# V's tiles at multiples of 64 bytes in place of 32 bytes behind them, in one layer of a hybrid encoder

## The chip, the core and the metric

The kernel runs on one core of one Trainium2 chip. The metric is the device time of one execution in microseconds (us). Five engines of the core are named as the profile names them: PE (TensorE, matmuls; PEld is its loading of the stationary operand, the "weights"), DVE (VectorE), ACT (ScalarE), POOL (GpSimd) and SP (SyncE, which here only issues DMAs).

## What is computed

One layer of an encoder over 512 tokens of width 2,048, in float32. One projection of the normalised input gives queries (8 heads of 128), keys and values (2 heads of 128, each shared by four query heads), two gates and the input of a linear recurrence. Attention and recurrence run beside each other; both are normalised, gated, joined and projected back.

```python
def hybrid_layer(x, norm_w, w_in, ...):
    h = rms_norm(x, norm_w)
    proj = jnp.einsum('bsd,de->bse', h, w_in)
    q, k, v, g_attn, xr, g_lru = jnp.split(proj, SPLITS, axis=-1)
    attn_out = attention_group(q, k, v, q_norm_w, k_norm_w)
    lru_out = lru_group(xr, conv_w, conv_b, ...)
    mixed = jnp.concatenate([rms_norm(attn_out, attn_norm_w) * jax.nn.silu(g_attn),
                             rms_norm(lru_out, lru_norm_w) * jax.nn.silu(g_lru)], axis=-1)
    return x + jnp.einsum('bse,ed->bsd', mixed, w_out)
```

What the change touches is the second product of attention, softmax weights times V:

```python
    def block(qb):
        s = jnp.einsum('bkgqd,bksd->bkgqs', qb.astype(jnp.float32), k_t.astype(jnp.float32)) * scale
        p = jax.nn.softmax(s, axis=-1)
        return jnp.einsum('bkgqs,bksd->bkgqd', p, v_t.astype(jnp.float32)).astype(q.dtype)
```

## The kernel before

**Matmuls in three parts.** A float32 operand is split into a high part, rounded to the matmul's narrower float type (fp32r, also four bytes in memory), and a low part, the rest. A product is then three matmuls, high x high, high x low, low x high, summed in PSUM. The helper `mm3` (lines 152 to 155) issues them, so most matmuls of the profile stand on lines 153, 154 and 155, and the tiles' names tell them apart. The last projection issues its own on line 1026.

**Stages.** PE's order is written out by hand for the whole kernel: projections fill the gaps of whatever chain runs beside them (`weave`, line 423). First comes the projection of the recurrence's input, with x being turned (up to about 50 us); then the recurrence in two halves, with the gate maps of `lru_pair` (line 493: `gh`, `gl`, loaded as weights, profile names `mm<-k,k`); then keys, values and queries are evacuated and rotated (`kv`, line 655, and `norm_rope`, line 600); then attention (`attention`, line 760) beside the projections of the gates (`pj<-x,wh` and `pj<-x,wl`); then the output's product (line 1026). ACT, DVE and POOL follow an order that the framework works out from the dependences of the tiles and from priorities, except in the first part of the first stage and in the last; SP's order is by hand in the first stage, in attention and in the last.

**V.** `kv` takes four tiles `kv` of 128 tokens x 512 (K's two heads, then V's). For each of them it makes a tile of V (lines 661 to 664) with the high part in its first 256 columns and the low part in the other 256; ACT writes the high part (line 665) and DVE the low (line 666). These tiles are read in one place, `values` (line 731): for a head, four blocks of 128 tokens, three matmuls each, twelve in all, with a 128 x 128 block of V as the weights and the turned softmax weights (`ph`, `pl`) streaming past. Eight heads make 96 matmuls, `mm<-ph,v` and `mm<-pl,v` in the profile. Between the heads lie the scores (`mm<-kt,q`, line 699) and the gates' projections.

**Where tiles lie.** SBUF is laid out in two stacks of pools per partition, one from the left and one from the right. The right stack holds, from its end downwards, a small `pad`, two rings, and then one after another `lru` (closed at line 1250), `qkv` (opened at line 1252; `ev`, `lq`, `kt`, V), under it `wx` (opened in `kv`, line 658; four `wh` and four `wl`) and, when that is closed, `att` (line 1268; `p`, `q`, `u`, `ph`, `pl`, `pt` and small tiles). A tile's first writer waits for the last readers of the older tiles that lay in the same bytes. The left stack of that time holds `rope` (`rq`, `rk`, `kv`) and `rot` (`rr`, `sh`, `sq` and others), which `att` later reaches over. The slots of `lru` named `k2` hold 2,048 bytes each.

`aside(tile_of, n)` (line 854) asks for a tile that is 16 floats longer than n x 256 and hands back a view that starts 8 floats (32 bytes) in. V is the only tile that is made with it.

Of the kernel before, what the change touches and what calls it, by code (L numbers as in the profile page):

```python
# [12 lines left out]
F32R = mybir.dt.float32r  # L13
# [4 lines left out]
P = 128  # L18
# [3 lines left out]
NT = SEQ // P  # L22
HD = 128
NH = 8
NKV = 2
# [23 lines left out]
H = 256  # L49
# [14 lines left out]
def hybrid_kernel(  # L64
# [25 lines left out]
    pools, order = {}, {"left": [], "right": []}  # L90

    def opened(name, side):
        pools[name] = tc.alloc_tile_pool(name=name, bufs=1, side=side, reuse_waits="tile")
        order[side].append(name)
        return pools[name]
# [22 lines left out]
    def nm(s):  # L118
        cnt[0] += 1
        return f"{s}_{cnt[0]}"  # L120
# [28 lines left out]
    def f(ap):  # L149
        return ap.bitcast(F32)  # L150
# [201 lines left out]
    def rows(dst, col, dg):  # L352

        shape = [P, NT, P]
        part = [const([P, NT], nm("part")) for _ in range(2)]
        parts = [dg() for _ in part]
        nc.vector.tensor_copy(part[0].bitcast(F32R), col)
        nc.vector.tensor_sub(part[1], col, part[0])
        for c, d in zip(part, parts):
            nc.vector.tensor_mul(  # L360
                d, ident[:, None, :].broadcast_to(shape), c[:, :, None].broadcast_to(shape)
            )
        yield
        pb = mm()
        for k, d in enumerate(parts):
            d = d.rearrange("p t q -> p (t q)")
            nc.tensor.matmul(pb, ones_r, d, start=k == 0, stop=k == 1)  # L367
        nc.vector.tensor_copy(dst, pb)
        yield
# [59 lines left out]
    def drain(fill):  # L429
        for _ in fill:  # L430
            pass
# [128 lines left out]
    def lru_squares():  # L560

        hsum = pools["rot"].tile([P, 2, SEQ], F32, tag="hsum", name="hsum")
        nc.scalar.activation(hsum, hp[0], AF.Square)
        for pair in hp[1:]:
            yield 2
            sq = pools["rot"].tile([P, 2, SEQ], F32, tag="hsq", bufs=1, name=nm("hsq"))
            nc.scalar.activation(sq, pair, AF.Square)
            nc.vector.tensor_add(hsum, hsum, sq)
        sums["l"] = hsum[:, 0, :]
        nc.gpsimd.tensor_add(sums["l"], sums["l"], hsum[:, 1, :])  # L570
# [29 lines left out]
    def norm_rope(es, nh, tab):  # L600

        es = [e[:, : nh * HD].rearrange("p (h d) -> p h d", d=HD) for e in es]
        rs = []
        for e in es:
            r = pools["rot"].tile([P, nh], F32, tag=f"rr{nh}", bufs=NT, name=nm("rr"))
            for h in range(nh):
                sq = pools["rot"].tile([P, HD], F32, tag="sh", bufs=1, name=nm("sh"))
                nc.scalar.activation(sq, e[:, h, :], AF.Square, accum_out=r[:, h : h + 1])
            rsqrt_mean(r, r, HD, nh)
            rs.append(r)  # L610
        for t, (e, r) in enumerate(zip(es, rs)):
            sq = pools["rot"].tile([P, nh, HD], F32, tag="sq", bufs=2, name=nm("sq"))
            nc.vector.tensor_mul(e, e, r[:, :, None].broadcast_to([P, nh, HD]))
            for s in range(2):
                nc.vector.tensor_mul(
                    sq.rearrange("p h (a s d) -> p h a s d", s=2, d=32)[:, :, :, s, :],
                    e.rearrange("p h (a s d) -> p h a s d", s=2, d=32)[:, :, :, 1 - s, :],
                    tab[:, t, 1, :].rearrange("p (a s d) -> p a s d", s=2, d=32)[:, None, :, s, :]
                    .broadcast_to([P, nh, 2, 32]),
                )  # L620
            nc.vector.tensor_mul(e, e, tab[:, t, 0, :][:, None, :].broadcast_to([P, nh, HD]))
            nc.vector.tensor_add(e, e, sq)
        return es
# [7 lines left out]
    def sent(es, nh, *us):  # L631

        us = us or [
            pools["rot"].tile([P, NQ, 2, NT, B], F32, tag="uq", bufs=2, name=nm("uq"))
            for _ in range(nh // 2)
        ]
        for n, u in enumerate(us):
            for t, e in enumerate(es):
                blocks(u, t, e[:, 2 * n : 2 * n + 2].rearrange("p h d -> p (h d)"))
            yield  # L640
            asides.append(put_aside(u, "qd", 5))

    def landed(aside_):

        to = pools["qkv"].tile([P, NQ, 2, NT, B], F32, tag="lq", bufs=2, name=nm("lq"))
        bring_back(to, aside_)
        return to

    def split_head(pair, k, hi, lo):
        src = pair[:, :, k]  # L650
        hi, lo = (in_order(v) for v in (hi, lo))
        nc.scalar.copy(hi, src)
        nc.vector.tensor_sub(lo, src, f(hi))

    def kv(es):
        turned_k = sent(norm_rope(es, NKV, rk), NKV)
        yield 20
        opened("wx", "right")
        for t in range(NT):
            vv = es[t][:, NKV * HD :]  # L660
            vt = aside(
                lambda *a: pools["qkv"].tile(*a, tag="v", bufs=NT, name=nm("v")), 2 * NKV * HD // H
            )
            vh[t], vl[t] = vt[:, 0, :], vt[:, 1, :]
            nc.scalar.copy(vh[t], vv)
            nc.vector.tensor_sub(vl[t], vv, f(vh[t]))
        yield from lru_squares()
        yield 2
        drain(turned_k)
        yield 6  # L670
        pair = landed(asides.pop(0))
        for h in range(NKV):
            yield (12, 4)[h]
            kt = pools["qkv"].tile([P, 2, SEQ], F32R, tag="kt", bufs=NKV, name=nm("kt"))
            kth[h], ktl[h] = kt[:, 0, :], kt[:, 1, :]
            split_head(pair, h, kth[h], ktl[h])
        r = group_rstd(sums["l"], "r_l", NB * P)
        yield 4
        drain(rows(
            gbc, r,  # L680
            lambda: pools["rope"].tile([P, NT, P], F32R, tag="kv", bufs=NT, name=nm("kv")),
        ))
# [133 lines left out]
    def group_rstd(src, name, n):  # L816

        pr = mm()
        for t in range(NT):
            nc.tensor.matmul(  # L820
                pr[:, t : t + 1], src[:, t * P : (t + 1) * P], ones[:, 0:1], start=True, stop=True
            )
        r = const([P, NT], name)
        nc.vector.tensor_copy(r, pr[:, :NT])
        rsqrt_mean(r, r, n, NT)
        return r
# [15 lines left out]
    def seven(pair, hi, lo):  # L842
# [7 lines left out]
        for to, part in ((slice(0, 3), src[:, 1:4]), (slice(3, 7), res)):  # L850
            nc.scalar.copy(hi[:, to], part)
            nc.vector.tensor_sub(lo[:, to], part, f(hi[:, to]))

    def aside(tile_of, n):

        t = tile_of([P, n * H + 16], F32R)
        return t[:, 8 : 8 + n * H].rearrange("p (n e) -> p n e", e=H)

    def kept(pool, i):
        return [  # L860
# [339 lines left out]
    for step in proj_feat(C_XR, a1, first, given):  # L1200
# [8 lines left out]
        c, e = step  # L1209
# [51 lines left out]

    fill = with_sums(both(), 3)
    weave(fill, kv(kvs))
    drain(fill)

# [171 lines left out]
```

## Time and profile before

| | |
|---|---|
| median of 3 runs | 631.11 us (630.88 to 631.38) |
| the profiled execution | 631.51 us |
| its span, first to last instruction | 629.7 us |
| mean granted PE clock in it | 0.998 |
| PE busy / PEld busy | 623.8 / 514.4 us |
| DVE / ACT / POOL busy | 491.2 / 348.5 / 104.0 us |
| DMA moved | 127.61 MB, mean 203 GB/s |

The span is what the profile shows of the execution; the rest of the execution's time lies around it. Busy shares are means over stages with different limits. A row of a group reads: line, engine, operation, tile written <- tiles read, shape, count, then busy time and the mean of one in ns. Matmuls overlap: a record's end is modelled and lies behind the start of the next, so the pace of matmuls is the distance of their starts. A weight load (PEld) runs beneath the matmul before the one that it is for.

### The profile page before, as it was taken

Reading aid. Unit: us, or ns where it says so; the run is one execution under the profiler, and the core shown is the slowest. Engines: PE = TensorE matmul, PEld = TensorE weight load, DVE = VectorE, ACT = ScalarE, POOL = GpSimd, SP = SyncE. Lnnn points to the kernel's source line nnn. Section 1 sums busy time; section 2 is a strip of 40 time slices with the busy share of each in tenths; the row PEclk is TensorE's granted clock in tenths of the full one; section 3 lists DMA queues with packets and bytes.
Section 4 is the critical chain, followed back from the end, with each engine's and each line's share of the span. In section 5 each row is a group of like instructions: output and inputs, shape, how many; then the busy total and the mean of one; then the engine's idle time right before and its main releaser. Section 6 shows DMA issues by size and latency. Waiting matters only on the chain.

```text
span 629.7 us, 8304 instructions
## 1 busy us (share of the span) xinstructions
PE 623.8 (99%) x2771; PEld 514.4 (82%) x2771; DVE 491.2 (78%) x796; ACT 348.5 (55%) x612; POOL 104.0 (17%) x137
## 2 busy tenths in 40 slices
PE   9999999999999999999999999999999999999997
PEld 6888888888888888888888888888888888888885
DVE  5967979986699874987887888549978866886875
ACT  3764899379936812555475447435445633443441
POOL 0000210112003631622122232100310001010010
PEclk9999999999999999999999999999999999999999
DMA  8877676859774599489668646924995777896262
GB/s 286 286 225 235 176 195 174 177 137 194 235 233 135 170 250 233 100 209 272 190 166 250 201 142 192 263 72 130 238 236 187 212 251 243 286 320 235 68 200 100
DMA packets 73594, 127.61 MB, mean 203 GB/s; under 512 B 6616, under 2 KB 29264, under 8 KB 73552
## 3 DMA queue, kind: packets, MB, share of 16 engines
q1 hardware_dynamic: 65664, 109.65, 55.7%
q0 software_dynamic: 7712, 17.31, 14.4%
q8 instruction: 21, 0.34, 0.2%
q10 hardware_dynamic: 176, 0.14, 0.1%
q14 instruction: 21, 0.17, 0.1%
HBM read 110.29 MB, written 37.75 MB: 235 GB/s over the span
## 4 chain that ended last, share of the span: by engine, by line
PE 97%; DMA 1%; DVE 0%; SPq 0%; ACT 0%; issue 0%; DVEq 0%
PE pj L154 21%; PE pj L153 20%; PE pj L155 20%; PE mm L1026 14%; PE pj L1026 10%; PE mm L155 4%; PE mm L153 3%; PE mm L154 3%; DMA wr<-in_w_in_dram 1%; PE mm L253 0%; PE mm L820 0%; PE mm L367 0%; SPq L240 0%; DVE wl L219 0%; DVE cb L1057 0%; SPq L206 0%
## 5 line engine op out<-in xcount | busy, mean ns | idle before, releaser
L153 PE MATMUL pj<-x,wh 128*128 128x512 f32 x376 | 146.9, 391 | 0.0
L154 PE MATMUL pj<-x,wh 128*128 128x512 f32 x376 | 146.6, 390 | 0.2 <-DVE x L261 0.2
L155 PE MATMUL pj<-x,wl 128*128 128x512 f32 x376 | 146.3, 389 | 0.0
L218 ACT CAST wh<-wr 128x512 fp32r<-128x512 f32 x143 | 85.6, 617 | 95.6 <-PE pj L154 36.7
L219 DVE TENSOR_TENSOR wl<-wr,wh 128x512 fp32r<-128x512 f32 x144 | 100.1, 722 | 20.0 <-ACT wh L218 18.7
L878 ACT CAST wh<-wr 128x1024 fp32r<-128x1024 f32 (+1 forms) x72 | 60.7, 860 | 75.0 <-PE mm L1026 35.4
L879 DVE TENSOR_TENSOR wl<-wr,wh 128x1024 fp32r<-128x1024 f32 (+1 forms) x72 | 68.7, 984 | 30.1 <-ACT wh L878 30.0
L154 PEld LDWEIGHTS pj<-x,wh 128*128 128x128 f32 x376 | 70.6, 188 | 15.2 <-DVE x L261 0.6
L155 PEld LDWEIGHTS pj<-x,wl 128*128 128x128 f32 x376 | 70.6, 188 | 14.8
L153 PEld LDWEIGHTS pj<-x,wh 128*128 128x128 f32 x376 | 70.6, 188 | 14.8
L153 PE MATMUL pj<-wh,x 128*128 128x512 f32 x192 | 74.8, 390 | 0.0
L155 PE MATMUL pj<-wh,x 128*128 128x512 f32 x192 | 74.7, 389 | 0.0
L154 PE MATMUL pj<-wl,x 128*128 128x512 f32 x192 | 74.7, 389 | 0.0
L902 POOL DMA_DIRECT2D t<-in_w_out_dram x40 | 33.7, 904 | 143.4 <-DMA t<-in_w_out_dram 99.9
L1026 PE MATMUL mm<-wh,ml 128*128 128x512 f32 x128 | 49.8, 389 | 0.0
L1026 PE MATMUL mm<-wh,mh 128*128 128x512 f32 x128 | 49.8, 389 | 0.0
L1026 PE MATMUL mm<-wl,mh 128*128 128x512 f32 x128 | 49.8, 389 | 0.0
L154 PEld LDWEIGHTS pj<-wl,x 128*128 128x128 f32 x192 | 36.0, 188 | 7.5
L153 PEld LDWEIGHTS pj<-wh,x 128*128 128x128 f32 x192 | 36.0, 188 | 7.5
L155 PEld LDWEIGHTS pj<-wh,x 128*128 128x128 f32 x192 | 36.0, 188 | 7.4
L708 POOL TENSOR_SCALAR p<-p,sm 128x512 f32<-128x512 f32 x32 | 24.2, 759 | 90.0 <-DVE sm L707 90.0
L1026 PE MATMUL pj<-wh,mh 128*128 128x512 f32 x96 | 37.4, 389 | 0.0
(209 smaller groups left out, 1035.6 us busy)
## 6 DMA issues: line engine op xcount, KB each, us to landing
wr<-in_w_in_dram SPq DMA_DIRECT2D x71, 512.0 KB, 5.0
wr<-in_w_out_dram SPq DMA_DIRECT2D x24, 512.0 KB, 5.3
t<-in_w_out_dram POOLq DMA_DIRECT2D x40, 256.0 KB, 7.3
wr<-t SPq DMA_DIRECT2D x40, 256.0 KB, 5.5
pd<-u SPq DMA_DIRECT2D x16, 512.0 KB, 3.0
pt<-pd SPq DMA_DIRECT2D x64, 128.0 KB, 3.9
t<-in_w_out_dram SPq DMA_DIRECT2D x24, 256.0 KB, 5.4
t<-t SPq DMA_DIRECT2D x16, 256.0 KB, 5.4
```

The costliest lines, as they stand in the source:

```text
L153: nc.tensor.matmul(acc, lh, rh, start=start, stop=False)
L154: nc.tensor.matmul(acc, lh, rl, start=False, stop=False)
L155: nc.tensor.matmul(acc, ll, rh, start=False, stop=stop)
L218: copy(hi, raw[:, k, :]).ins,
L219: nc.vector.tensor_sub(lo, raw[:, k, :], f(hi)).ins,
L708: last_pool[0] = nc.gpsimd.tensor_scalar(p, p, sm, 0.0, op0=ALU.mult, op1=ALU.add).ins
L878: nc.scalar.copy(hi[:, to], b)
L879: nc.vector.tensor_sub(lo[:, to], b, f(hi[:, to]))
L902: nc.gpsimd.dma_start(dst, src, accum_op=ALU.add)
L1026: nc.tensor.matmul(dst[s], lh[:, ts_], rh, start=i == 0 and j == 0, stop=i == 7 and j == 2)
```

## The change

V's four tiles are asked for directly as 128 x 2 x 256 floats in the pool `qkv`, without the 16 extra floats and without the 32 bytes ahead of the data. The helper `aside`, which nothing else uses, goes.

```diff
         for t in range(NT):
             vv = es[t][:, NKV * HD :]
-            vt = aside(
-                lambda *a: pools["qkv"].tile(*a, tag="v", bufs=NT, name=nm("v")), 2 * NKV * HD // H
-            )
+            vt = pools["qkv"].tile([P, 2, NKV * HD], F32R, tag="v", bufs=NT, name=nm("v"))
             vh[t], vl[t] = vt[:, 0, :], vt[:, 1, :]
...
-    def aside(tile_of, n):
-
-        t = tile_of([P, n * H + 16], F32R)
-        return t[:, 8 : 8 + n * H].rearrange("p (n e) -> p n e", e=H)
-
```

## The prediction

> **What bounds the kernel now.** I read the page first: how the span divides between engines, and the chain that ended last.
>
> ```profile
> span 629.7 us, 8304 instructions
> ...
> PE 623.8 (99%) x2771; PEld 514.4 (82%) x2771; DVE 491.2 (78%) x796; ACT 348.5 (55%) x612; POOL 104.0 (17%) x137
> ...
> PE 97%; DMA 1%; DVE 0%; SPq 0%; ACT 0%; issue 0%; DVEq 0%
> ```
>
> The tensor engine's matmuls fill 99% of the span and 97% of the chain. Next I asked for its waits; this is the whole answer for that engine:
>
> ```profile
> PE mm L1144 <- POOL ones L161: 1.1, 1, 1.1
> PE pj L154 <- DVE x L261: 0.2, 1, 0.2
> ```
>
> Both belong to the beginning: the warm-up matmuls of L1144 and the first columns of x (L261). From there on one matmul follows another, so a change can move the end in only two ways: it alters the pace of matmuls, or it makes the tensor engine wait where it does not wait now. The pace in an undisturbed stretch is best read from merged pieces of the chain, here one of the last product's:
>
> ```profile
> 569.29 2.72 PE pj L1026 x12
> ```
>
> 2.72 / 12 = 0.2267 us per matmul. A single matmul is recorded with 389 ns, because its recorded end lies 162 ns behind the start of the next; what a matmul is recorded longer than 389, it holds up the next. Then the groups of V's products and of the scores in the attention stretch alone (302 to 421 us), the only one in which V is read (the last columns are busy us and mean ns of one, then idle time before):
>
> ```profile
> L153 PE MATMUL mm<-ph,v 128*128 128x512 f32 x32 | 12.7, 397 | 0.0
> L154 PE MATMUL mm<-pl,v 128*128 128x512 f32 x32 | 12.6, 394 | 0.0
> L155 PE MATMUL mm<-ph,v 128*128 128x512 f32 x32 | 12.6, 394 | 0.0
> L155 PE MATMUL mm<-kt,q 128*128 128x512 f32 x22 | 8.6, 391 | 0.0
> L154 PE MATMUL mm<-kt,q 128*128 128x512 f32 x22 | 8.6, 389 | 0.0
> L153 PE MATMUL mm<-kt,q 128*128 128x512 f32 x21 | 8.2, 389 | 0.0
> ```
>
> The products with V are the slow ones: 397, 394 and 394 ns against 389. The scores' third matmul (kt,q, L155) has 391 where its two sisters have 389. The timeline of one head shows why. The first row is a weight load, the others are matmuls (start, duration):
>
> ```profile
> 301.97 0.19 PEld L153 LDWEIGHTS mm<-ph,v 128*128 128x128 f32 x1
> ```
> ```profile
> 301.97 0.40 PE L155 MATMUL mm<-kt,q 128*128 128x512 f32 x1
> 302.20 0.39 PE L153 MATMUL mm<-ph,v 128*128 128x512 f32 x1
> ...
> 305.23 0.40 PE L154 MATMUL pj<-x,wh 128*128 128x512 f32 x1
> ...
> 306.85 0.39 PE L155 MATMUL pj<-x,wl 128*128 128x512 f32 x1
> ...
> 308.21 0.39 PE L155 MATMUL mm<-kt,q 128*128 128x512 f32 x1
> ```
>
> The load of the first V block runs beneath the scores' last matmul, and that matmul, which reads no V at all, is already a long one. So the disturbance comes with loading V as weights, not with streaming P. It also outlasts V: pj matmuls at 305.23 are still 0.40. From 301.97 to 306.85 there are 21 matmuls (one of the scores, twelve of V, eight of pj) in 4.88 us; from 306.85 to 308.21 there are six in 1.36 us, the undisturbed 0.2267 again.
>
> **What sets V apart.** The pools tell it. The qkv pool is laid downwards from byte 196,544 (3,071 x 64): kt 2 x 4,096, lq 2 x 4,096, ev 4 x 2,048, then V's four tiles. With `aside` these are 528 floats (2,112 = 33 x 64 bytes) from 163,520 on, and the operand starts 32 bytes in. Every other operand of the matmuls named so far lies in a slot whose size is a multiple of 2,048 and whose start is a multiple of 64. V alone starts 32 past one.
>
> **The change part by part.**
>
> *V's operand address.* V's four tiles become 2,048 bytes each at 163,776 + 2,048n, with no offset. The lru pool is laid from the same byte 196,544: ev 4 x 2,048, then twelve k2 slots down to exactly 163,776. V's new places are therefore the lowest four of the k2 slots, from which the gate maps were loaded as weights earlier in this same run, and all twelve slots have one phase. Their matmuls:
>
> ```profile
> L153 PE MATMUL mm<-k,k x32: 389/389/389, 63.3 to 157.8; 128*128 128x512 f32 x32
> L154 PE MATMUL mm<-k,k x32: 389/389/389, 63.5 to 158.1; 128*128 128x512 f32 x32
> L155 PE MATMUL mm<-k,k x32: 389/389/389, 63.8 to 158.3; 128*128 128x512 f32 x32
> ```
>
> 389 is the least, the median and the most of all 96. That is the nearest row for V after the change, so I take 389 for its matmuls.
>
> The sum for one head: 21 matmuls now take 4.88 us and would take 21 x 0.2267 = 4.76, a gain of 0.12 us; for eight heads 0.96 us. Smaller bound: if only V's own matmuls recover and the edges before and behind them do not, (8 + 5 + 5) ns x 32 = 0.58 us. Larger bound: the least duration in the rows below for an aligned fp32r matmul is 387, two ns under the usual; 168 matmuls x 2 ns would add 0.34, hence 1.30 us. Below nothing too: nothing excludes that aligned V collides with the P stream in some new way; if it costs as much more as it costs now, the loss is 0.96 us. I take 0.96 of gain, because the k,k rows are the same addresses.
>
> ```profile
> L155 PE MATMUL pj<-x,wl x376: 387/389/397, 14.2 to 472.3; 128*128 128x512 f32 x188
> ```
>
> [...]
>
> *Writing V.* Four casts (L665) and four subtractions (L666) write V. The subtraction takes 419 ns, and one of the same shape from and into aligned tiles 418, so there is nothing to gain:
>
> ```profile
> L666 DVE TENSOR_TENSOR v<-kv,v x4: 418/419/422, 186.7 to 199.0; 128x256 fp32r<-128x256 f32 x4
> L621 DVE TENSOR_TENSOR kv<-kv,rk x4: 418/418/418, 192.0 to 199.3; 128x256 f32<-128x256 f32 x4
> ```
>
> They end over 100 us before V is first read (302.20), which hides them; in the open they would be 4 x 0.42 us.
>
> *The tiles behind V.* V's pool shrinks by 4 x 64 = 256 bytes, so the pools stacked under it (wx, later att) move up by 256. That is a multiple of 64, so no phase changes, but it changes which older tiles a slot lies over, and with that what its first writer waits for. V and wx now lie on whole slots of lru, so they wait for fewer. In att four slots come to reach over a tile that they did not touch: the first p slot over rk, the top one (112,064 to 114,112) over a kv slot last read by the matmuls of L367, the first q slot over another kv slot, the second (118,208 to 122,304) over K's rr and over sh. The latest readers among these are L367 and L608, and both are done before att is first written:
>
> ```profile
> L367 PE MATMUL mm<-kv,ones_r x2: 392/392/393, 238.3 to 238.6; 128*128 128x512 f32 x2
> ```
> ```profile
> 258.16 0.30 ACT L608 ACTIVATE sh<-ev 128x128 f32<-128x128 f32 x1
> ...
> 263.80 1.14 ACT L652 CAST q<-lq 128x512 fp32r<-128x512 f32 x2
> ```
>
> I cost this at nothing: L608's last pass over sh ends at 258.5, and the q cast runs at 263.80. No instruction or DMA is added or removed, and the queues keep their work.
>
> **The sum.** The profiled execution took 631.51 us (span 629.70 and 1.81 around it), 0.40 above the median of the runs, 631.11. 631.51 - 0.96 = 630.55 for such an execution; against the median 631.11 - 0.96 = 630.15, which I round to 630.2.
>
> **The rivals.**
>
> *It is not the 32 bytes.* Then nothing moves: 631.1. For it: the load itself is no longer for V than elsewhere, and the sums in asum, which start 32 past a multiple of 64 as well (byte 9,312), load as fast as those in hsum, which do not:
>
> ```profile
> L155 PEld LDWEIGHTS mm<-ph,v x32: 187/187/192, 302.4 to 420.3; 128*128 128x128 f32 x32
> ```
> ```profile
> L820 PEld LDWEIGHTS mm<-ones,asum x8: 188/192/192, 430.1 to 431.0; 128*128 128x128 f32 x8
> ```
> ```profile
> L820 PEld LDWEIGHTS mm<-ones,hsum x8: 187/192/192, 231.7 to 232.6; 128*128 128x128 f32 x8
> ```
>
> Against it: those loads run beside one-column matmuls, with no long stream to disturb, and the k,k products show that the same shape at aligned places has no such cost. [...] Chance 0.17.
>
> *Aligned V collides with P.* Both would start at multiples of 64. Price 0.96 us, so 632.1; it would count as slower from 1.26 / 168 = 7.5 ns per matmul. Against it: k,k, kt,q and x,wh have both operands so, at 389. Chance 0.06.
>
> *The end on the other side: the q pair comes later.* The one place behind the start where the tensor engine is late is the first attention scores. Their third matmul needs the low part of q, which the vector engine makes behind two weight splits:
>
> ```profile
> 265.89 1.29 DVE L219 TENSOR_TENSOR wl<-wr,wh 128x512 fp32r<-128x512 f32 x2
> 267.09 1.29 DVE L653 TENSOR_TENSOR q<-lq,q 128x512 fp32r<-128x512 f32 x2
> ```
> ```profile
> 267.83 0.50 PE L155 MATMUL mm<-kt,q 128*128 128x512 f32 x1
> ```
>
> That matmul has 0.50 in place of 0.39, a stall of 0.11. Both q slots are among those that reach over something new, and the program's order on this engine is worked out from such dependences. Each pair of splits that comes to stand ahead of q adds about 1.2 us of stall (265.89 to 267.09), paid in full. One pair eats the gain (631.11 - 0.96 + 1.20 = 631.35), and from two pairs it is slower: 631.11 - 0.96 + 2.40 = 632.6. Against it: what q newly waits for (sh, the latest) is over 5 us earlier than its cast. Chance 0.09.
>
> **How the numbers follow.** The forecast has 0.68. Runs of the kernel before lie within 0.5 us of each other, and I take 0.2% (1.26 us) as what can be told from no change. The forecast's gain is under that, its larger bound just over: I give 0.20 of the 0.68 to faster and 0.48 to same. The first rival is same (0.17); of the second, half is same and half slower; of the third 0.02 is same and 0.07 slower. Together faster 0.20, same 0.70, slower 0.10. The range runs from the larger bound, 631.11 - 1.30 = 629.8, up over the smaller bound (630.5) and no change to 631.4, the case of one pair; what is above or below has about 0.2.
>
> **What would show it.** Right: the ph,v and pl,v groups at 389, the scores' L155 at 389 in the stretch of attention, about 4.76 us over the 21 matmuls from the first V load, and other stretches as long as before. Wrong: V's groups unchanged at 394 to 397 (the first rival), above 400 (the second), a kt,q matmul near 268 us with much more than 0.50 (the third). Any other stretch whose length changes by over 0.3 us would mean that the order or the waits moved, which this sum leaves out.

## The result and the profile after

| | before | after |
|---|---|---|
| median of 22 runs | 631.24 us (630.82 to 632.94) | 630.2 us (629.76 to 631.43) |
| the profiled execution | 631.51 us | 630.62 us |
| its span | 629.7 us | 628.8 us |

The ratio of after to before is 0.9981, with a 95% interval of 0.9975 to 0.9986: about 1.2 us less (0.9 to 1.6). The two medians lie 1.04 us apart.

The page of the kernel after, span and busy times, and the groups of V's products and of the scores in the stretch from 302 to 421 us:

```profile
span 628.8 us, 8304 instructions
...
PE 622.7 (99%) x2771; PEld 514.2 (82%) x2771; DVE 490.9 (78%) x796; ACT 348.1 (55%) x612; POOL 104.6 (17%) x137
```
```profile
L153 PE MATMUL mm<-ph,v 128*128 128x512 f32 x32 | 12.5, 390 | 0.0
L154 PE MATMUL mm<-pl,v 128*128 128x512 f32 x32 | 12.5, 390 | 0.0
L155 PE MATMUL mm<-ph,v 128*128 128x512 f32 x32 | 12.5, 390 | 0.0
L155 PE MATMUL mm<-kt,q 128*128 128x512 f32 x22 | 8.6, 390 | 0.0
```

The same instructions in the same order on every engine, with 1.1 us less of busy matmul time. V's groups went from 397, 394 and 394 ns to 390 (the prediction had 389). The timeline of the first head, from the matmul beneath which the first V block is loaded:

```profile
301.63 0.39 PE L155 MATMUL mm<-kt,q 128*128 128x512 f32 x1
301.86 0.39 PE L153 MATMUL mm<-ph,v 128*128 128x512 f32 x1
...
306.39 0.39 PE L155 MATMUL pj<-x,wl 128*128 128x512 f32 x1
```

These 21 matmuls take 4.76 us (before: 4.88). Where the span's 0.9 us lies is read from two places where a sum over partitions is taken, hsum ahead of attention and asum behind it:

```profile
L818 PEld LDWEIGHTS mm<-ones,hsum x8: 188/192/193, 231.4 to 232.3; 128*128 128x128 f32 x8
```
```profile
L818 PEld LDWEIGHTS mm<-ones,asum x8: 188/192/192, 428.8 to 429.7; 128*128 128x128 f32 x8
```

Ahead of attention this execution is 0.33 us earlier (231.72 to 231.39), of which all lies in the first 50 us (the first matmul with `ones_r`, behind the sum over x, starts at 50.09 us in place of 50.42, 0.33 earlier too) and nothing with V; behind attention it is 1.28 us earlier (430.10 to 428.82). So attention gave 0.95 us. Near the end 0.35 us go back. First two pieces of the chain, then the timeline:

```profile
604.82 6.55 DMA wr<-in_x_dram
612.62 1.74 DVE wl L872 x2
```
```profile
616.81 0.39 PE L1019 MATMUL pj<-wh,mh 128*128 128x512 f32 x1
617.28 0.50 PE L1019 MATMUL pj<-wl,mh 128*128 128x512 f32 x1
617.62 0.40 PE L1019 MATMUL pj<-wh,ml 128*128 128x512 f32 x1
```

Two starts lie 0.47 and 0.34 us apart instead of 0.227, a stall of 0.35 us. The chain runs back from there over the weight splits of DVE to a load of x for the residual. The kernel before had no such stall in its profile. Of the ten experiments below only two have one here (0.5 us with V's slots kept, 0.14 us with 16 bytes in place of 32). Whether it comes and goes with the kernel or with the execution is not shown; no run was made on it. The first 50 us differ as much without any reason in V: with the projections' weights left alone, the profiles of the experiments have them from 0.3 us shorter to 0.4 us longer than the kernel after.

### The profile page after: what moved, and what is told of

It is laid out like the page before. It is cut to its first block, busy times and chain, and to the rows that moved or that the text cites. A ratio compares the mean times of both kernels' runs of the same rounds, so it can differ in the third digit from the quotient of the medians.

```text
span 628.8 us, 8304 instructions
## 1 busy us (share of the span) xinstructions
PE 622.7 (99%) x2771; PEld 514.2 (82%) x2771; DVE 490.9 (78%) x796; ACT 348.1 (55%) x612; POOL 104.6 (17%) x137
## 4 chain that ended last, share of the span: by engine, by line
PE 94%; DMA 2%; DVE 2%; SPq 0%; issue 0%; ACT 0%; POOL 0%; DVEq 0%; POOLq 0%; ACTq 0%
PE pj L154 21%; PE pj L155 21%; PE pj L153 20%; PE mm L1019 12%; PE pj L1019 9%; PE mm L155 3%; PE mm L154 3%; PE mm L153 3%; DMA wr<-in_w_in_dram 1%; DMA wr<-in_x_dram 1%; DVE wl L872 1%; PE mm L253 0%; DVE xt L1096 0%; PE mm L818 0%; PE mm L367 0%
## 5 line engine op out<-in xcount | busy, mean ns | idle before, releaser
L1019 PE MATMUL pj<-wl,mh 128*128 128x512 f32 x96 | 37.5, 391 | 0.1
```

What stands on the lines that cost most here:

```text
L1019: nc.tensor.matmul(dst[s], lh[:, ts_], rh, start=i == 0 and j == 0, stop=i == 7 and j == 2)
```

## The experiments

Every edit is made to the kernel after. From here on places are given modulo 256 bytes (the remainder when the byte address is divided by 256), since that turned out to be what orders them. The streams ph, pl, kt and x lie at 192 in both kernels, and so do the operands of all other long runs of matmuls; only the constants and the sums lie elsewhere. V's four tiles, in the order in which a head reads them, lay at 224, 160, 96 and 32 before (slots of 2,112 bytes drift by 64), and lie at 192 after.

**V's slots kept, only the 32 bytes gone.** The first test of the prediction's own reason, called the first theory below: a load of weights that starts off a multiple of 64 bytes costs.

```diff
-            vt = pools["qkv"].tile([P, 2, NKV * HD], F32R, tag="v", bufs=NT, name=nm("v"))
+            vt = pools["qkv"].tile([P, 2 * NKV * HD + 16], F32R, tag="v", bufs=NT, name=nm("v"))
+            v0 = 0
+            vt = vt[:, v0 : v0 + 2 * NKV * HD].rearrange("p (n e) -> p n e", n=2)
```

> V's slots stay 2,112 bytes at their old places (163,520 + 2,112n), and so does everything stacked under them; only the 32 bytes ahead of the data go, so that the operand starts at a multiple of 64. Theory (the start address of the weights costs): V's groups at 389 to 390 ns, 21 matmuls from the first V load in 4.76 us, the median about 0.96 us under the kernel before and as fast as the kernel after (ratio to before 0.998 to 0.9988). Rival (the 256 bytes by which wx and att moved, or V's new slots, brought it): V's groups stay at 394 to 397 ns and the ratio is 1.000.

Measured: 630.84 us, ratio to before 0.9993 (0.9984 to 1.0002), where the kernel after has 0.9981: no clear gain. V's groups have 394 ns, though every tile starts at a multiple of 64. The timeline shows which of the twelve are slow:

```profile
301.32 0.39 PE L155 MATMUL mm<-kt,q 128*128 128x512 f32 x1
301.54 0.39 PE L153 MATMUL mm<-ph,v 128*128 128x512 f32 x1
301.77 0.39 PE L154 MATMUL mm<-pl,v 128*128 128x512 f32 x1
302.00 0.39 PE L155 MATMUL mm<-ph,v 128*128 128x512 f32 x1
302.22 0.39 PE L153 MATMUL mm<-ph,v 128*128 128x512 f32 x1
302.45 0.39 PE L154 MATMUL mm<-pl,v 128*128 128x512 f32 x1
302.68 0.40 PE L155 MATMUL mm<-ph,v 128*128 128x512 f32 x1
302.92 0.40 PE L153 MATMUL mm<-ph,v 128*128 128x512 f32 x1
```

The first V tile (192 modulo 256) is loaded without cost: the three matmuls from 301.32 on, beneath which its blocks are loaded, take 0.68 us, 3 x 0.2267. In this head the second (128) costs nothing either: the next three, from 302.00 on, take 0.68 us as well. The long matmuls begin at 302.68, beneath which the first block of the third (64) is loaded, and stay for the fourth (0): the seven distances from 302.68 to 304.32 make 1.64 us where 7 x 0.2267 are 1.59. The first theory falls. The rival (the moved pools) does not explain why the first tile is free.

**16 bytes in place of 32, in the old slots** (`vt[:, 4 : 4 + 2 * NKV * HD]`; the tiles at 208, 144, 80 and 16).

> V's slots as before, the data 16 bytes in (not 32). Theory (a load that starts off a multiple of 64 costs, whatever the offset): V's groups 394 to 398 ns as before, about 631.2 us. Rival (what counts is a multiple of 16, or 32 is special): 389 to 390 ns, about 630.2 us.

V's groups have 393, 394 and 393 ns; the time was 631.83 us in a single run. Here too the first tile, 16 bytes from 192, cost nothing and the other three did: the starts of the first head's matmuls lie 227, 226, 227 ns apart for it, then 230, 234, 227, 232 and more. Neither the first theory nor its rival had foreseen a difference between tiles.

**V and its streams 32 bytes in** (V as before, ph and pl in tiles of 2,064 floats from the eighth on).

> V 32 bytes past a multiple of 64 as before, and ph and pl, which stream past it, too. Theory (only where the weights start counts): V's groups still 394 to 398 ns or more, about 631.2 us. Rival (what counts is that weights and stream have different phases): 389 to 390 ns inside each group of twelve, the scores' last matmul, beneath which the first V block is loaded, still near 397; about 630.5 us.

V's groups have 394, 394 and 392 ns; the time was 632.47 us in a single run. For V this answers less than was meant: the longer tiles put ph at 96 and pl at 160, not at 224, so V and its streams were still apart in most pairs. The surprise is in the scores, of which nothing was changed but the place (the longer ph and pl pushed q down by 128 bytes, from 192 to 64):

```profile
L153 PE MATMUL mm<-kt,q 128*128 128x512 f32 x22 | 8.9, 404 | 0.0
L155 PE MATMUL mm<-kt,q 128*128 128x512 f32 x22 | 8.7, 396 | 0.0
L154 PE MATMUL mm<-kt,q 128*128 128x512 f32 x22 | 8.7, 395 | 0.0
```

q and kt are both at multiples of 64, and the scores are slow. From this and the two runs before came the second theory: what counts is the place of the weights against that of the stream above which they are loaded, modulo 256.

**The projections' split weights 32 bytes in** (wh and wl in slots of 2,112 bytes, read from the eighth float on; V as after).

> V at multiples of 64, and instead the split weights wh and wl of all projections but the last 32 bytes past one (slots 64 bytes longer). In six of the nine projections they are loaded as weights (pj<-x,wh and pj<-x,wl: 1,152 matmuls), in three they stream (pj<-wh,x: 576). Theory: every load costs what one of V's twelve cost, 0.96 us / 96 with the tail or 6.6 ns without it, so the pj<-x rows go from 389 to about 396 ns and the time up by 7.6 to 11.5 us, to 638 to 642 us. The pj<-wh,x rows stay at 389. Rival (it is peculiar to V's products): pj<-x rows at 389, 630.2 us.

Slots of 2,112 bytes drift here as V's did, so each pair of weights and stream is 32 or 96 bytes apart. Measured: 641.25 us, ratio 1.0155 (1.0141 to 1.0169), 11 us over the kernel after. So the cost is not peculiar to V. But where they stream, too, the split weights cost, which the first theory had excluded. First the kernel after, then this one:

```profile
L153 PE MATMUL pj<-x,wh 128*128 128x512 f32 x376 | 146.9, 391 | 0.0
L153 PE MATMUL pj<-wh,x 128*128 128x512 f32 x192 | 74.9, 390 | 0.0
```
```profile
L153 PE MATMUL pj<-x,wh 128*128 128x512 f32 x376 | 148.8, 396 | 0.0
L154 PE MATMUL pj<-x,wh 128*128 128x512 f32 x376 | 148.6, 395 | 0.0
L153 PE MATMUL pj<-wh,x 128*128 128x512 f32 x192 | 76.0, 396 | 0.0
L154 PE MATMUL pj<-wl,x 128*128 128x512 f32 x192 | 75.9, 395 | 0.0
```

In pj<-wh,x the weights are x, still at a multiple of 64, and the moved wh streams. So the weights' own place is not enough to tell what costs; the pair of places is what the next run tests.

**All operands moved by 32 bytes.** The test of the second theory against the first: 8 more floats at the end of the constants move the left stack up, 56 more in `pad` move the right one down, and every operand that was at 192 is at 224.

```diff
-    opened("pad", "right").tile([P, 8], F32, name="pad")
+    opened("pad", "right").tile([P, 64], F32, name="pad")
...
     gbc = const([P, SEQ], "gbc")
+    const([P, 8], "shift")
```

> The kernel after, with both stacks moved so that every operand that lay at 192 modulo 256 (V, ph, pl, q, kt, the gate maps, x, wh, wl, mh, ml) lies at 224, 32 bytes past a multiple of 64. First theory (a load that starts off a multiple of 64 costs): all 2,600 matmuls near 394 to 397 ns, some 15 us more, 645 us. Second theory, formed on the two looks before (what counts is the place of the weights against that of the stream above them, modulo 256): every pair is still at difference 0, all rows at 389, the time that of the kernel after, ratio to before 0.998.

Measured: 630.25 us, ratio 0.9983 (0.9974 to 0.9991), as the kernel after. Attention:

```profile
L153 PE MATMUL mm<-ph,v 128*128 128x512 f32 x32 | 12.5, 389 | 0.0
L154 PE MATMUL mm<-pl,v 128*128 128x512 f32 x32 | 12.5, 389 | 0.0
L155 PE MATMUL mm<-ph,v 128*128 128x512 f32 x32 | 12.5, 389 | 0.0
L153 PE MATMUL mm<-kt,q 128*128 128x512 f32 x21 | 8.2, 389 | 0.0
```

V lies 32 bytes past a multiple of 64, as in the kernel before, and is at full pace. The first theory would have had 15 us more.

**V at a multiple of 64, and 64 bytes from its streams** (slots of 2,304 = 9 x 256 bytes, the data from the sixteenth float on, so all four tiles at 0).

> V's slots 2,304 bytes (9 x 256), the data 64 bytes in: all four V tiles at multiples of 64, and at 0 modulo 256 where the streams are at 192. First theory: 389 to 390 ns. Second theory (difference modulo 256, here 64): V's groups 393 to 397 ns, about 631 us; a difference of 64 was slow in about half of its undisturbed cases so far, so 391 to 394 is possible too.

```profile
L154 PE MATMUL mm<-pl,v 128*128 128x512 f32 x32 | 12.7, 396 | 0.0
L153 PE MATMUL mm<-ph,v 128*128 128x512 f32 x32 | 12.7, 396 | 0.0
L155 PE MATMUL mm<-ph,v 128*128 128x512 f32 x32 | 12.6, 395 | 0.0
```

V's groups have 395 and 396 ns, with 631.56 us in one run: as the second theory has it, and against the first.

**One of V's four tiles 32 bytes off** (slots of 2,304, the offset only for `t == 0`).

> V's slots 2,304 bytes, three tiles at 192 modulo 256 and the first tile alone 32 bytes further, so that 24 of the 96 loads are out of phase, the first three of each head. If only a load out of phase costs: 24 x 6.6 ns = 0.16 us over the kernel after, matmuls 4 to 12 of each head at 389. If a disturbance outlasts its cause by eight to nine matmuls, as behind V in the kernel before: matmuls 4 to 12 near 394 as well, about 12 x 4 to 6 ns per head, 0.4 to 0.6 us, and the pj matmuls behind V at 389.

```profile
301.92 0.40 PE L155 MATMUL mm<-kt,q 128*128 128x512 f32 x1
302.15 0.39 PE L153 MATMUL mm<-ph,v 128*128 128x512 f32 x1
302.38 0.39 PE L154 MATMUL mm<-pl,v 128*128 128x512 f32 x1
...
303.77 0.39 PE L154 MATMUL mm<-pl,v 128*128 128x512 f32 x1
```

The starts from the first load on lie 235, 231, 229, then 231, 236, 228, 233, 231, then 227 ns apart and less: three loads out of phase and five matmuls behind them that read only tiles in phase. Eight intervals take 1.854 us where 8 x 0.2267 are 1.814, 0.04 us; over eight heads 0.3 us, between the two expectations. A disturbance outlasts its cause, by five matmuls here.

**The remaining operands at 192 too** (pads of 16, 8 and 40 floats among the constants ahead of `ident`, ahead of `asum` and behind it, and one of 32 floats ahead of `hsum`).

> The kernel after, with the constants ident, ones, ones_r and the sums asum and hsum moved to 192 modulo 256 too, so that no large operand of the tensor engine is out of phase. If the remaining long matmuls of the kernel after (near 50 to 54, 231 to 239, 429 to 436 us) come from these loads, they fall to 389 and up to 0.3 us goes (ratio to before 0.9975 to 0.998). Rival (they come from the kind of matmul, one column or plain float32): no change against the kernel after, 0.998.

Measured: 630.2 us, ratio 0.9989 (0.998 to 0.9998), no different from the kernel after. The rows do show the effect, on the matmuls with `ones_r` that spread a row over the partitions; first the kernel after, then this one:

```profile
L367 PE MATMUL mm<-k,ones_r x2: 392/393/394, 50.1 to 50.3; 128*128 128x512 f32 x2
```
```profile
L368 PE MATMUL mm<-k,ones_r x2: 389/389/389, 49.9 to 50.1; 128*128 128x512 f32 x2
```

With the matmuls behind them that makes some 0.1 us in all, too little for the time to tell; part of the long matmuls at these places stays, so the rival has a share too. No version clearly beats the kernel after.

**V 16 and V 32 bytes off, without drift** (slots of 2,304; all four tiles at 208, and at 224).

> V's slots 2,304 bytes (9 x 256), the data 16 bytes in: all four tiles at 208 modulo 256, no multiple of 32 or 64, and 16 bytes from the streams' 192. First theory (off a multiple of 64 costs): 394 to 398 ns. Second theory (difference modulo 256) with a small difference taken as free, as for the first V tile of the run with 16 bytes before: 389 to 390 ns in all three V groups and about 630.2 us.

> The same slots, the data 32 bytes in: all four tiles at 224 modulo 256. Both theories expect long V groups, 394 to 398 ns, and the scores' third matmul near 391 in the stretch from 302 to 421 us, about 631.2 us. It gives the cost of the 32 bytes without the drift that slots of 2,112 bytes bring; if it is far under 0.96 us over the kernel after, the drift made a part of the cost of the kernel before.

First 16 bytes, then 32:

```profile
L153 PE MATMUL mm<-ph,v 128*128 128x512 f32 x32 | 12.5, 390 | 0.0
L154 PE MATMUL mm<-pl,v 128*128 128x512 f32 x32 | 12.5, 390 | 0.0
L155 PE MATMUL mm<-ph,v 128*128 128x512 f32 x32 | 12.5, 390 | 0.0
```
```profile
L155 PE MATMUL mm<-ph,v 128*128 128x512 f32 x32 | 12.7, 396 | 0.0
L154 PE MATMUL mm<-pl,v 128*128 128x512 f32 x32 | 12.6, 395 | 0.0
L153 PE MATMUL mm<-ph,v 128*128 128x512 f32 x32 | 12.6, 395 | 0.0
L155 PE MATMUL mm<-kt,q 128*128 128x512 f32 x22 | 8.6, 391 | 0.0
```

At 16 bytes V costs next to nothing (630.66 us in one run), though its start is no multiple of 32; at 32 bytes it costs (630.88 in one run). Two single runs so close tell nothing by their times; the starts of the matmuls do. Summed over the distances from one start to the next of at least 229 ns from 300 to 425 us, what exceeds 226.7 is 0.97 us in the kernel before, 0.69 us with a uniform 32 bytes, 0.69 us in the old slots without the 32 bytes, 0.09 us with a uniform 16 bytes and 0.03 us in the kernel after. So the 32 bytes alone cost 0.69 us, and the drift of the old slots alone costs 0.69; together they made 0.97.

## Why the prediction was right, and where its reason was not

- *The bound.* Right: matmuls make up 97% of the chain before and 94% after, and the pace of matmuls is all that is seen to change with V's place.
- *The step, V's operand address, 0.12 us a head and 0.96 us in all.* Right in place and size: 4.88 to 4.76 us over 21 matmuls, and 0.97 - 0.03 = 0.94 us over attention. The forecast of 630.2 is the median measured; that it agrees to the tenth is partly luck, since the kernel before has 631.24 over 22 runs where the prediction had 631.11, and the other stretches moved too. The smaller bound (0.58, V's own matmuls alone) would have missed the tail behind V, which the run with one tile off shows by itself.
- *"V alone starts 32 past one."* Wrong as a reason. It was true and it is not what counts: with all operands 32 past a multiple of 64 nothing in attention is slow (V's groups 389 ns), with V at 64 bytes from its streams V is (395 and 396), and at 16 it is not (390). What sets V apart is its place against the streams', modulo 256. The step held because its evidence, the k,k rows, was at the very addresses that V took; these are in phase with everything else (at the same place modulo 256), so they could not tell one reason from the other. That V's streams ph and pl lie at that phase too was not looked at, so that the pace of k,k carried over to V was in this respect luck. The drift of the 2,112-byte slots, which the prediction wrote down (163,520 + 2,112n), was passed over.
- *Writing V.* Right at nothing: the copies stayed as they were (the casts 389 to 392 ns before and after, the subtractions 418 to 422 before and 419 to 420 after) and hidden.
- *The tiles behind V.* Right: DVE's program has the same order of operations in both kernels, and no wait was added at the scores near 268 us: their third matmul has 0.50 us in both kernels. The rival there did not happen.
- *The rival "it is not the 32 bytes".* It expected no gain. Its doubt was sound, its conclusion not: V's place is the cause, only measured from another mark. Yet taken by its words it was nearer the truth than its chance of 0.17: with the 32 bytes gone and the slots kept, 0.69 of the 0.97 us stay, and only the new slot size takes them away.
- *What the sum left out.* The first 50 us differ by 0.3 us between the two profiles and the end by a stall of 0.35 us; they cancel in this pair. Both are over the 0.3 us that the prediction had named as a sign that the order or the waits had moved: the order did not, the wait at the end is new in this profile, and its cause is open. The ratio's interval holds the predicted gain of 0.96.

## What to carry to other kernels

Where fp32r matmuls of this shape run back to back, lay the operands that meet as weights and stream at the same place modulo 256 bytes, and make slots multiples of 256, so that they do not drift apart: 1,728 matmuls out of phase cost 11 us here. When a row shows that a new place is good, ask in how many ways it differs from the old one; the run that moves everything by the suspected amount tells an operand's own place from its place against the others. And count what follows a disturbed instruction, not it alone.

## What the runs showed of the hardware that was not expected

- In these runs the pace of the fp32r matmuls with 512 columns depends on the distance between the weights being loaded and the operand streaming meanwhile, modulo 256 bytes. Counted over the two kernels and the first eight experiments, for matmuls behind at least six undisturbed ones: at distance 0 there are some 21,900 cases, mean 226.7 ns from start to start, and a few dozen of them have 229 or more, most at the same places of several runs (the first 25 us, near 267, 334, 552 and 617 us). With the weights 32 bytes further than the stream it was 235 ns (20 cases), at 128 bytes apart 232.6 (over 30 cases, all slow); at 64 bytes either way about half were slow, and what decides there is open; 16 bytes further was free (24 cases, mean 227.0). Other distances were met too seldom to say.
- That the number is 256 and no larger one shows when all twelve kernels are counted in this way: among the pairs at distance 0, those an odd multiple of 256 bytes apart (over 4,000) have 226.7 to 226.9 ns from start to start, no more than the others.
- A weight load keeps its 187 to 188 ns in nearly all of these cases (V's 96 in the kernel before have 187 to 192); it is the matmul above it that grows.
- Behind V's last load out of phase it takes two to nine matmuls to come back to 226.7 ns: nine in the kernel before, seven in its slots without the 32 bytes, five with one tile off, two with all four tiles 32 bytes off.
- Why 256 bytes, and why 16 are free, is open: no run here looks inside the memory or the engine.
